# A list scheduler's durations, landing times and DMA order in a hybrid attention block

## The chip, the cores and the metric

The kernel runs on one core of one Trainium2 chip. The metric is the device time of one execution in microseconds (us). Three runs of the kernel before gave 1061.60, 1064.79 and 1065.99 us; their median is 1064.79 us.

## The reference

One layer of a streaming encoder over 16 meta tokens and 512 frames of width 1024, in float32. The stream is normalised and multiplied by one wide matrix `w_in`; its columns feed two token mixers that run beside each other, eight heads each. What follows is cut to what is computed:

```python
proj = layer_norm(h) @ w_in                       # 1024 x 7704
q_a,k_a,v_a,f_a, q_b,k_b,v_b, a_b,b_b,z_b, gate_a,gate_b = split(proj)
# FoX: softmax attention, head dim 64, with a cumulative forget gate
logits = q_a @ k_a.T * 64**-0.5 + cum[:, None] - cum[None, :]     # cum = cumsum(log_sigmoid(f_a + b_f))
y_a = softmax(causal(logits)) @ v_a
# gated DeltaNet (GDN), head dim 128: conv of 4 taps, silu, l2 norm of q and k, then by chunks
a = strict_lower((k*beta) @ k.T * decay)          # decay = exp(gc_i - gc_j)
u, w = solve(I + a, v*beta), solve(I + a, k*beta*exp(gc))
for chunk: v_new = u - w @ state; o = q_dec @ state + attn @ v_new; state = state*g_last + k_dec.T @ v_new
y_b = rms_norm(o) * gdn_norm_w * silu(z_b)
mixed = sigmoid(gate_a) * (y_a @ w_out_a) + sigmoid(gate_b) * (y_b @ w_out_b)
h = layer_norm(ALPHA*h + mixed @ w_o)
h = layer_norm(ALPHA*h + (silu(h @ w_gate) * (h @ w_up)) @ w_down)
```

## The kernel before

**Units.** The input projection is cut into units of 128 columns of `w_in`, named after what they make: f (the gate rows of all heads), qN, kN, vN and zN of GDN head N, qaP, kaP, vaP of the FoX head pair P, and last gaI, gbI, the output gates. The units run on TensorE in a fixed order (lines 66 and 1163 to 1179): group 0 has k0 q0 f0 z0 v0 z1 k1 q1 v1 and then qa0 ka0 va0; the later groups have k, q, v, k, q, v, qa, ka, va, z, z.

**A unit's weight.** Float32 is computed as three fp32r products: x_hi and x_lo with the high part of the weight, then x_hi with its low part. Unit u's raw weight (`wr_`) is loaded by SyncE (SP) into one of three buffers; ScalarE casts it to the high part (`wh_`) and writes its negative into the low part (`wl_`); then GpSimd (POOL) issues a DMA that adds the raw weight onto `wl_`. In unit u the load of u + 3 is issued at its first step and the split of u + 1 starts at its second (the hook, lines 1266 to 1271). The low pass comes last in a unit and needs `wl_` landed.

**Side work.** Between a unit's steps the planner puts the steps of the side tasks, Python generators that yield what they wait for: the scan of the gates (ending in `rows_d` in DRAM), per GDN head `gdn_prepare` (transposes psk, psq, psm, square sums, the norm chain on VectorE, Gram products) and `gdn_decay` (row broadcasts ea and em read back from `rows_d`, masked on GpSimd by AFFINE_SELECT), per group of two heads `gdn_invert` (a substitution of 31 steps on VectorE, written to DRAM as td and read back as tm and pm), `gdn_chunk` and `gdn_finish` (GpSimd's product o), the conv taps (c_q, c_k, c_v), the FoX heads, and the gates (tg). `reload` reads the pairs y_b0 and y_b2 back from DRAM; `y_tiles` then holds the split of the mixers' outputs (ys_) for the out projections.

**What sets the order.** The planner keeps a clock per engine, `est_t`. `account` (line 168) moves it on by `spent` (line 150) for every instruction, and notes when each tile is written and read; a DMA lands `DMA_LAT + fine[0]` later. `tick` (line 627) takes the side task that is ready by these clocks, within `LOOK` and `BUSY`, until `CAP` us of TensorE are placed. `Ordered` (line 199) wraps each engine: it calls `account`, and keeps the instruction in the order in which the program is written if its engine is in `PINS` and it is not a DMA:

```python
if pinned[0] and self.name in PINS and op != "dma_start":
    tc.keep_in_program_order(ins)
```

What isn't kept so is placed by the compiler's scheduler, by its own priorities; the masks of `affine_select` and the loads and casts after the units (resid, ys_, wr_wo) are placed by it too, in both kernels.

Of the kernel before, what the change touches and what calls it, by code (L numbers as in the profile page):

```python
# [8 lines left out]
F32 = mybir.dt.float32  # L9
# [6 lines left out]
PSUM = bass.MemoryType.PSUM  # L16
DRAM = bass.MemoryType.DRAM

P = 128
# [16 lines left out]
BLK = 32  # L36
BPITCH = BLK * P + BLK

PINS = ("pe", "act", "dve", "pool")
PIN_FROM = 0  # L40
LOOK, MARGIN, CAP = 0.4, 1.0, 0.6
BUSY = {'dve': 3.0, 'act': 1.0}
LAT, SELF, DMA_LAT, DMA_FINE = 0.15, 0.13, 2.3, 2.5
RAW, SPLIT, ADD_LAT = 3, 2, 3.0
HF, LOAD_ORDER = 4, "0m1pk23q"


# [16 lines left out]

STORE_AT = 3
ORDERS = "k0 q0 f0 z0 v0 z1 k1 q1 v1 x0", "k0 q0 v0 k1 q1 v1 x0 z0 z1"
SPLIT_AT = 1
POOL_BIAS = 1.2
TAIL_AT = 1
ON_POOL, AFFINE_AT = False, 14  # L70
# [7 lines left out]
def hybrid_block(ctx, tc, x, meta_tokens, ln_in_g, ln_in_b, w_in, b_f, conv_w, a_log, dt_bias,  # L78
# [16 lines left out]

    est_t = dict.fromkeys(("pe", "act", "dve", "pool", "sp"), 0.0)
    wrote, read, ring = {}, {}, {}
    fine, stale = [0.0], set()

    def tname(v):  # L100
        t = getattr(v, "tensor", None)
# [47 lines left out]

    def spent(eng, op, out, src, many):  # L150
        if op == "dma_start":
            return 0.05
        n = free(out)
        if eng == "pe":
            if op == "transpose":
                return 2 * max(n, P) / 2400
            return (4 if src[0].dtype == F32 else 1) * max(n, free(src[0])) / 2400
        n = max([n] + [free(v) for v in src[:1]])
        if op == "memset":
            return 0.05 + 1e-3 * n  # L160
        if eng == "act" and many:
            return 0.17 + 0.85e-3 * n
        if eng == "pool":
            return 0.15 + (2.1e-3 if op.startswith("tensor") else 1e-3) * n
        n += 60 if any(v.space == PSUM for v in src[:2]) else 0
        return {"act": 0.09 + 0.85e-3 * n, "dve": 0.068 + 1.04e-3 * n}[eng]

    def account(eng, op, a, k):
        aps = [v for v in list(a) + list(k.values()) if tname(v)]
        outs = [aps[0]] + ([k["accum_out"]] if "accum_out" in k else [])  # L170
        src = [v for v in aps[1:] if v is not k.get("accum_out")]
        assert not any(tname(v) in stale for v in aps), [tname(v) for v in aps]
        begin = est_t[eng]
        for v in src:
            begin = max(begin, after(wrote, tname(v), eng, 0.0 if eng == "pe" else SELF))
        for v in outs:
            if wrote.get(tname(v), (0.0, ""))[1] != "sp" or eng != "sp":
                begin = max(begin, after(wrote, tname(v), eng), after(read, tname(v), eng))
        end = begin + spent(eng, op, outs[0], src, len(outs) > 1)
        if op == "dma_start":  # L180
            done = end + DMA_LAT + fine[0]
        else:
            done = est_t[eng] = end
        for v in outs:
            wrote[tname(v)] = max(done, wrote.get(tname(v), (0.0, ""))[0]), eng
        for v in src:
            if read.get(tname(v), (0.0, ""))[0] < done:
                read[tname(v)] = done, eng
# [10 lines left out]
    class Ordered:  # L199
# [3 lines left out]
        def __getattr__(self, op):  # L203
            fn = getattr(self.eng, op)

            def call(*a, **k):
                ins = fn(*a, **k)  # L207
                account(self.name, op, a, k)
                if pinned[0] and self.name in PINS and op != "dma_start":
                    tc.keep_in_program_order(ins)  # L210
                return ins
            return call
# [476 lines left out]
    def gdn_decay(hd):  # L689
        h = hd["h"]  # L690
        ea = gp.tile([P, NT, 2, P], F32, tag="ea", name=f"ea{h}", bufs=4)
        for i in range(2):
            src = rows_d[(1 + i) * HEADS + h, META:].rearrange("(c n) -> c n", n=P)
            sp.dma_start(ea[:, :, i, :], src.unsqueeze(0).broadcast_to([P, NT, P]))
        em = gp.tile([META, META], F32, tag="em", name=f"em{h}", bufs=2)
        sp.dma_start(em, rows_d[HEADS + h, :META].unsqueeze(0).broadcast_to([META, META]))
        yield at(rdy(ea, em), 0, "act")
        yield lambda: not busy
        busy.append(h)
        eq = gp.tile([P, NT, P], F32, tag="eq", name=f"eq{h}", bufs=1)  # L700
        act.activation(eq, ea[:, :, 1, :], AF.Exp)
        for i, op in ((0, ALU.is_gt), (1, ALU.is_ge)):
            pool.affine_select(ea[:, :, i, :], ea[:, :, i, :], [[0, NT], [1, P]], op, NEG,
                               base=0, channel_multiplier=-1)
        pool.affine_select(em, em, [[1, META]], ALU.is_gt, NEG, base=0, channel_multiplier=-1)
        yield at(rdy(ea, em), 0, "act")
        for c in range(NT):
            act.activation(ea[:, c], ea[:, c], AF.Exp, bias=neg_gc[:, c, h:h + 1])
            yield soon("act")
        act.activation(em, em, AF.Exp, bias=neg_gc[:META, 4, h:h + 1])  # L710
        hd["ea"], hd["em"], hd["eq"] = ea, em, eq
# [85 lines left out]
    def gdn_invert(g, st):  # L797
# [25 lines left out]
        sp.dma_start(td[0], t3)  # L823
        dve.tensor_copy(n3, t3.rearrange("p a b -> p b a"))
        sp.dma_start(td[1], n3)
        tv = td[:, :32].rearrange("w (i b) r n -> w b r i n", b=4)
        fine[0] = DMA_FINE
        for b, c in ((0, 0), (1, 32), (2, 0)):
# [411 lines left out]
    for u, d in enumerate(units):  # L1240
        pinned[0] = u >= PIN_FROM
        if u == STORE_AT:
            for t in range(NT):
                sp.dma_start(h_v[:, t, :], toks[t])
        if u - 2 in finishing:
            gen, ps = finishing.pop(u - 2)
            finish_now(gen, lambda: tname(ps) in freed)
        if d["name"].startswith("qa"):
            pr = int(d["name"][2:])
            drain(lambda: not pr or fox[pr - 1]["done"] == 3)  # L1250
        def low():
            if u in splitting:
                finish_now(splitting.pop(u), lambda: u in los)
            return los[u]

        ps = outs0[d["name"]] if u < 2 else gbanks(f"ps_{d['name']}")
        outs = [ps[:, i, :b - a] for i, (a, b) in enumerate(d["cols"])]
        passes = [(outs, d["cols"])]
        if u == 0:
            passes = []  # L1260
            load_unit(u + 3)
            start_split(u + 1)
        elif u == 1:
            passes = [(outs[1:], d["cols"][1:])]
        for n, (o, c) in enumerate(passes):
            def hook(j):
                if n == 0 and j == 0:
                    load_unit(u + 3)
                if n == 0 and j == SPLIT_AT:
                    start_split(u + 1)  # L1270
                tick()
            if d["name"] == "f":
                o, low = [v[:6 * HEADS] for v in o], None
            gemm(o, his[u], low, x_hi, x_lo, c, KT, hook)
        gen = d["finish"](ps)
        finishing[u] = gen, ps
        start(gen, 0)
        advance(side[-1])
# [585 lines left out]
```

## Time and profile before

| what | value |
|---|---|
| median of three runs | 1064.79 us (1061.60 to 1065.99) |
| profiled execution: time, span, granted clock | 1062.41 us, 1060.7 us, 0.987 |
| busy TensorE (PE) | 989.1 us, 93% |
| busy VectorE (DVE) | 694.9 us, 66% |
| busy ScalarE (ACT) | 504.4 us, 48% |
| busy GpSimd (POOL) | 335.4 us, 32% |
| DMA | 131.03 MB, 124 GB/s on average |
| chain that ended last | PE 51%, DVE 24%, DMA 9%, issue 8%, ACT 5%, POOL 2% |

The time is that of the whole execution, the span goes from its first to its last instruction. PE busy for 93% says that it stands still for 7% of the span. The chain is followed back from the last instruction, at each step to what released it. A granted clock of 1.0 is TensorE's upper level (2.4 GHz), 0.5 its lower one (1.2 GHz). The units run from 31 to 560 us; out projections, the first layer norm, the FFN and the last norm follow.

### The profile page before, as it was taken

The numbers are of one execution on the slowest core, as the hardware profiler recorded it, in microseconds if no ns is written. First come the engines' busy times: TensorE is split into PE (matmuls) and PEld (weight loads), VectorE is DVE, ScalarE is ACT, GpSimd is POOL, SyncE is SP. The second block draws the span as 40 slices with busy tenths as digits, with TensorE's granted clock in tenths as the row PEclk, the third lists the DMA queues.
The fourth block names the chain that finished last, engine by engine and source line by source line (L and its number), as shares of the span: only waits on it lengthen the run. The fifth ranks groups of instructions, "written<-read, shape, count | busy, mean of one in ns | idle before, by whom it ended". The sixth has DMA issues, their size and how long they took to land.

```text
span 1060.7 us, 17731 instructions
## 1 busy us (share of the span) xinstructions
PE 989.1 (93%) x6765; PEld 881.9 (83%) x6765; DVE 694.9 (66%) x1467; ACT 504.4 (48%) x1031; POOL 335.4 (32%) x359
## 2 busy tenths in 40 slices
PE   5988999999989899999999999879999999999995
PEld 4887998779878898876877887679999999988884
DVE  6446586369837884780246546788989998964435
ACT  6466667455744577544463224434444435531121
POOL 5213211212130223011028002674555645235005
PEclk9999999999989999999999999999999999999998
DMA  7587656537653576457685335104243342344222
GB/s 222 132 181 168 141 111 129 135 67 173 155 122 69 125 179 140 105 138 173 162 214 151 111 100 159 41 2 118 80 120 105 95 120 81 100 136 142 84 77 79
DMA packets 170577, 131.03 MB, mean 124 GB/s; under 512 B 19708, under 2 KB 151068, under 8 KB 170492
## 3 DMA queue, kind: packets, MB, share of 16 engines
q1 hardware_dynamic: 161788, 98.39, 33.0%
q0 software_dynamic: 8704, 31.51, 15.6%
q8 instruction: 53, 0.87, 0.3%
q14 instruction: 32, 0.26, 0.1%
HBM read 90.90 MB, written 8.57 MB: 94 GB/s over the span
## 4 chain that ended last, share of the span: by engine, by line
PE 51%; DVE 24%; DMA 9%; issue 8%; ACT 5%; POOL 2%; SPq 0%; DVEq 0%; POOLq 0%; ACTq 0%
PE d L1366 3%; PE d L1364 3%; PE d L1365 3%; PE ps_v L207 3%; DVE wlo_b L1428 3%; PE ptm L207 3%; PE ps_ga L207 2%; PE ps_q L207 2%; PE ps_z L207 2%; PE ps_gb L207 2%; PE ps_va L207 2%; DMA wl_ga<-wr_ga 2%; PE po L1321 2%; PE o L240 2%; PE po L1319 2%
## 5 line engine op out<-in xcount | busy, mean ns | idle before, releaser
L285 DVE TENSOR_TENSOR wl_d<-wr_d,wh_d 128x1024 fp32r<-128x1024 f32 x18 | 29.6, 1643 | 45.2 <-ACT wh_d L283 45.2
L283 ACT CAST wh_d<-wr_d 128x1024 fp32r<-128x1024 f32 x18 | 18.9, 1050 | 66.5 <-PE d L1366 44.6
L1482 POOL TENSOR_TENSOR wr_a<-wr_a,sums 128x512 f32<-128x512 f32 x22 | 29.2, 1329 | 66.3 <-DVE wl_a L1428 66.2
L207 DVE TENSOR_TENSOR t<-t,tmp 34x31 f32<-34x31 f32 (+15 forms) x124 | 42.8, 345 | 2.1 <-DVE tmp L207 0.2
L207 DVE TENSOR_TENSOR tmp<-n,t 34x31 f32<-34x31 f32 (+15 forms) x124 | 41.9, 338 | 2.8 <-DMA n<-nd 0.9
L1476 POOL TENSOR_TENSOR sums<-wr_a,spare_raw 128x512 f32<-128x512 f32 x11 | 14.7, 1335 | 81.4 <-DVE stats L240 70.9
L1365 PE MATMUL d<-wl_d,f_h 128*128 128x512 f32 (+1 forms) x104 | 39.7, 381 | 0.0
L1364 PE MATMUL d<-wh_d,f_h 128*128 128x512 f32 (+1 forms) x104 | 39.6, 381 | 0.0
L1448 PE MATMUL pa<-v_h,wh_a 128*128 128x256 f32 x160 | 39.3, 279 | 0.0
L1448 PE MATMUL pa<-v_h,wl_a 128*128 128x256 f32 x160 | 39.1, 279 | 0.0
L1667 ACT ACTIVATE res<-res 128x512 f32<-128x512 f32 x11 | 7.0, 634 | 62.1 <-DVE res L1728 62.1
L240 POOL TENSOR_SCALAR rst_l<-rsy_l,ve_l 128x1 f32<-128x1 f32 x21 | 10.8, 514 | 73.0 <-DVE rsy_l L240 71.6
L1428 DVE TENSOR_TENSOR wlo_b<-wr_b,whi_b 128x1024 fp32r<-128x1024 f32 x11 | 22.6, 2054 | 16.4 <-ACT whi_b L1427 16.4
L283 ACT CAST wh_wo<-wr_wo 128x512 fp32r<-128x512 f32 (+1 forms) x16 | 13.3, 836 | 40.9 <-PE po L1320 13.8
L285 DVE TENSOR_TENSOR wl_wo<-wr_wo,wh_wo 128x512 fp32r<-128x512 f32 (+1 forms) x16 | 22.3, 1405 | 15.8 <-ACT wh_wo L283 15.8
L1448 PEld LDWEIGHTS pa<-v_h,wh_a 128*128 128x128 f32 x160 | 30.2, 188 | 0.0
L1448 PEld LDWEIGHTS pa<-v_h,wl_a 128*128 128x128 f32 x160 | 30.0, 187 | 0.0
L207 DVE SCALAR_TENSOR_TENSOR r<-ks,nbeg,bv 128x128 f32<-128x128 f32 x32 | 11.2, 351 | 28.6 <-PE ks L207 23.4
L207 ACT COPY o<-ks 128x128 f32<-128x128 f32 x32 | 8.5, 266 | 44.2 <-DVE r L207 44.2
L1448 PE MATMUL px<-v_h,rb 128*128 128x256 f32 x176 | 25.5, 289 | 2.9 <-ACT v_h L240 2.9
L1448 PE MATMUL px<-v_h,wlo_b 128*128 128x256 f32 x88 | 22.7, 293 | 5.8 <-DVE wlo_b L1428 5.8
L1427 ACT CAST whi_b<-spare_raw 128x1024 fp32r<-128x1024 f32 x10 | 10.5, 1052 | 35.4 <-PE pd L1448 35.4
(791 smaller groups left out, 3696.7 us busy)
## 6 DMA issues: line engine op xcount, KB each, us to landing
wr_d<-in_w_down_dram SPq DMA_DIRECT2D x18, 512.0 KB, 3.8
spare_raw<-in_w_gate_dram SPq DMA_DIRECT2D x11, 512.0 KB
wr_b<-in_w_up_dram SPq DMA_DIRECT2D x11, 512.0 KB, 3.9
wr_a<-in_w_gate_dram SPq DMA_DIRECT2D x11, 512.0 KB
wr_a<-in_w_up_dram SPq DMA_DIRECT2D x11, 512.0 KB, 5.6
wr_k<-in_w_in_dram SPq DMA_DIRECT2D x8, 512.0 KB, 7.0
wr_q<-in_w_in_dram SPq DMA_DIRECT2D x8, 512.0 KB, 4.3
wr_z<-in_w_in_dram SPq DMA_DIRECT2D x8, 512.0 KB, 5.7
```

Source lines behind the costliest of these rows:

```text
L207: ins = fn(*a, **k)
L240: return lambda *a, **k: tc.keep_in_program_order(fn(*a, **k))
L283: nc.scalar.copy(hi[:, :k * n], raw[:, :k * n])
L285: eng.tensor_sub(lo[:, :k * n], raw[:, :k * n], hi[:, :k * n].bitcast(F32))
L1319: nc.tensor.matmul(g[:, j, :], wh[:, i, :], hi[i], start=i == 0, stop=False)
L1321: nc.tensor.matmul(g[:, j, :], wl[:, i, :], hi[i], start=False, stop=i == k - 1)
L1364: nc.tensor.matmul(acc, ah, wh[:, cols], start=kk == 0, stop=False)
L1365: nc.tensor.matmul(acc, ah, wl[:, cols], start=False, stop=False)
L1366: nc.tensor.matmul(acc, al, wh[:, cols], start=False, stop=kk == ktiles - 1)
L1428: order(eng.tensor_sub(lo, src, hi.bitcast(F32)))
L1448: order(nc.tensor.matmul(dst, a[:, k, :], v[i][:, k, :], start=n == 0, stop=n == 11))
L1482: pin(nc.gpsimd.tensor_sub(v1[:, 1], v1[:, 1], sums[:, 0]))
```

## The change

The constants, the two duration functions, the place of a load in its unit, the list of engines held in program order, one wait and one landing time are changed:

```diff
-PINS = ("pe", "act", "dve", "pool")
+PINS = ("pe", "act", "dve", "pool", "sp")
-LAT, SELF, DMA_LAT, DMA_FINE = 0.15, 0.13, 2.3, 2.5
-RAW, SPLIT, ADD_LAT = 3, 2, 3.0
+LAT, SELF, DMA_LAT, DMA_FINE, DMA_ROWS, SWITCH = 0.15, 0.02, 2.3, 3.2, 6.0, 0.1
+RAW, SPLIT, ADD_LAT = 3, 2, 3.4
-SPLIT_AT = 1
+SPLIT_AT, LOAD_AT = 1, 12
     def spent(eng, op, out, src, many):
         if op == "dma_start":
-            return 0.05
+            return 0.85 if eng == "pool" else 0.45
         n = free(out)
         if eng == "pe":
+            full = op == "transpose" or src[0].dtype == F32
+            switch = SWITCH if full != pe_full[0] else 0.0
+            pe_full[0] = full
             if op == "transpose":
-                return 2 * max(n, P) / 2400
-            return (4 if src[0].dtype == F32 else 1) * max(n, free(src[0])) / 2400
+                return switch + max(n, P) / 1175
+            return switch + (2 * max(n, free(src[0])) / 1150 if full else max(n, free(src[0])) / 2195)
         n = max([n] + [free(v) for v in src[:1]])
         if op == "memset":
-            return 0.05 + 1e-3 * n
-        if eng == "act" and many:
-            return 0.17 + 0.85e-3 * n
+            return 0.05 + 0.9e-3 * n
+        if eng == "act":
+            return (0.28 if many else 0.09) + 0.9e-3 * n
         if eng == "pool":
-            return 0.15 + (2.1e-3 if op.startswith("tensor") else 1e-3) * n
-        n += 60 if any(v.space == PSUM for v in src[:2]) else 0
-        return {"act": 0.09 + 0.85e-3 * n, "dve": 0.068 + 1.04e-3 * n}[eng]
+            return 0.15 + (2.1e-3 if op.startswith("tensor_t") or op in ("tensor_add", "tensor_sub", "tensor_mul") else 1e-3) * n
+        return 0.14 + 1.0e-3 * n
...
         if op == "dma_start":
             done = end + DMA_LAT + fine[0]
+            est_t[eng] = end
...
-                if pinned[0] and self.name in PINS and op != "dma_start":
+                if pinned[0] and self.name in PINS:
                     tc.keep_in_program_order(ins)
...
             src = rows_d[(1 + i) * HEADS + h, META:].rearrange("(c n) -> c n", n=P)
+            fine[0] = DMA_ROWS
             sp.dma_start(ea[:, :, i, :], src.unsqueeze(0).broadcast_to([P, NT, P]))
+            fine[0] = 0.0
...
         sp.dma_start(td[1], n3)
+        yield at(rdy(td) - MARGIN)
...
-                if n == 0 and j == 0:
+                if n == 0 and j == LOAD_AT:
                     load_unit(u + 3)
```

So the DMAs that the planner issues on SyncE and GpSimd are kept in the order of the program, those clocks move on with each, and all its other choices are made with the new durations. What this does to the order of the instructions is shown at four places (the number at a name's end only tells tiles apart).

GpSimd from the adding DMA of z1's weight on, before (wl_ is a weight's low part, ea0 to ea2 the decay tiles of heads 0 to 2, gt3 a scratch tile of the gates, nm0 a small tile of head 0):

```order
L207 DMA wl_z1_596<-wr_z1_462 128x1024
L207 MEMSET gt3_523 128x120
L207 DMA wl_k1_676<-wr_k1_517 128x1024
L207 AFFINE_SELECT ea0_706<-ea0_706 128x4x128
L207 AFFINE_SELECT em0_709<-em0_709 16x16
L207 DMA wl_q1_760<-wr_q1_591 128x1024
L207 AFFINE_SELECT ea1_1011<-ea1_1011 128x4x128
L207 AFFINE_SELECT ea0_706<-ea0_706 128x4x128
L207 AFFINE_SELECT em1_1014<-em1_1014 16x16
L207 DMA wl_v1_866<-wr_v1_670 128x1024
L207 MEMSET nm0_930 32x32
L207 AFFINE_SELECT ea2_1678<-ea2_1678 128x4x128
```

and after (qf0 is the query tile of head 0):

```order
L210 DMA wl_z1_594<-wr_z1_496 128x1024
L210 MEMSET gt3_520 128x120
L210 AFFINE_SELECT ea0_682<-ea0_682 128x4x128
L210 DMA wl_k1_721<-wr_k1_574 128x1024
L210 AFFINE_SELECT em0_685<-em0_685 16x16
L210 DMA wl_q1_765<-wr_q1_621 128x1024
L210 AFFINE_SELECT ea0_682<-ea0_682 128x4x128
L210 DMA wl_v1_866<-wr_v1_736 128x1024
L210 MEMSET nm0_926 32x32
L210 DMA wl_qa0_942<-wr_qa0_820 128x1024
L210 TENSOR_TENSOR qf0_500<-qf0_500,eq0_832 128x512
L210 AFFINE_SELECT ea1_1005<-ea1_1005 128x4x128
```

One mask of ea0 has moved ahead of the adding DMA of k1, the masks of ea1 have moved behind that of qa0, and those of ea2 are no longer among these rows.

TensorE around the transposes of head 4, before (psk4, psm4 and psq4 are banks of PSUM, ps_q5 that of unit q5):

```order
L207 MATMUL ps_q5_3234<-x_lo_128,wh_q5_3149 128x268 x2
L207 MATMUL ps_q5_3234<-x_hi_127,wh_q5_3149 128x268 x2
L207 MATMUL psk4_3286<-ident_107,k4T_3067 128x128 x4
L207 MATMUL psm4_3288<-ident_107,k4T_3067 16x128
L207 MATMUL psq4_3287<-ident_107,qf4_3154 128x128 x4
L207 MATMUL ps_q5_3234<-x_lo_128,wh_q5_3149 128x268 x2
```

and after (ps_k5 is the bank of unit k5, which runs ahead of q5):

```order
L210 MATMUL ps_k5_3160<-x_hi_127,wh_k5_3091 128x268 x2
L210 MATMUL ps_k5_3160<-x_lo_128,wh_k5_3091 128x268 x2
L210 MATMUL psk4_3216<-ident_107,k4T_3087 128x128 x4
L210 MATMUL psm4_3218<-ident_107,k4T_3087 16x128
L210 MATMUL psq4_3217<-ident_107,qf4_3156 128x128 x4
L210 MATMUL ps_k5_3160<-x_hi_127,wh_k5_3091 128x268 x2
```

The transposes have moved forward by one unit.

SyncE around the reload of the mixer's output (y_b0_again, y_b2_again), before:

```order
L207 DMA wr_gb0_5274<-in_w_in_dram 128x8x128
L207 DMA wr_ga1_5485<-in_w_in_dram 128x8x128
L207 DMA wr_gb1_5674<-in_w_in_dram 128x8x128
L207 DMA y_b0_again_6570<-y_d_132 128x1024
L207 DMA y_b2_again_6572<-y_d_132 128x1024
L207 DMA wr_ga2_5752<-in_w_in_dram 128x8x128
```

and after (wr_wo is a weight of the out projections, resid the residual stream):

```order
L210 DMA wr_gb6_6349<-in_w_in_dram 128x8x128
L210 DMA wr_ga7_6419<-in_w_in_dram 128x8x128
L1310 DMA resid0_6620<-h_d_129 128x1024
L210 DMA wr_gb7_6464<-in_w_in_dram 128x8x128
L210 DMA y_b0_again_6570<-y_d_132 128x1024
L210 DMA y_b2_again_6572<-y_d_132 128x1024
L275 DMA wr_wo0_0_6639<-in_w_out_a_dram 128x4x128
L1310 DMA resid2_6628<-h_d_129 128x1024
L275 DMA wr_wo1_0_6657<-in_w_out_b_dram 128x8x128
```

The two loads have moved from between the gate weights gb1 and ga2 to behind the last one, gb7.

ScalarE near the end of the units, before (tg12 is the tanh of the gate unit ga6, ys_ the split outputs):

```order
L207 CAST wh_gb6_6438<-wr_gb6_6299 128x1024
L207 ACTIVATE wl_gb6_6439<-wh_gb6_6438 128x1024
L1296 CAST ys_o_14_6591<-y_b6_5487 128x512
L207 ACTIVATE tg12_6479<-ps_ga6_6433 128x512
L207 CAST wh_ga7_6482<-wr_ga7_6364 128x1024
L1296 CAST ys_pm_12_6590<-y_b6_5487 128x512
L207 ACTIVATE wl_ga7_6483<-wh_ga7_6482 128x1024
```

and after:

```order
L210 CAST wh_gb6_6448<-wr_gb6_6349 128x1024
L1302 CAST ys_o_14_6591<-y_b6_5521 128x512
L210 ACTIVATE wl_gb6_6449<-wh_gb6_6448 128x1024
L1302 CAST ys_qf_0_6580<-y_b0_again_6570 128x512
L210 ACTIVATE tg12_6479<-ps_ga6_6445 128x512
L210 CAST wh_ga7_6482<-wr_ga7_6419 128x1024
L1302 CAST ys_kt_2_6582<-y_b0_again_6570 128x512
L210 ACTIVATE wl_ga7_6483<-wh_ga7_6482 128x1024
L1302 CAST ys_kn_4_6584<-y_b2_again_6572 128x512
```

Two casts of the reloaded tile y_b0_again now stand between the split of gb6 and that of ga7, one of them ahead of the tanh of ga6.

## Rows read from the trace of the kernel before

**Rows 1.** Window (us, engines' busy us (xcount), PEclk, DMA share, GB/s), the planned stretch

```profile
31.00:560.00 529.00, 497.45 (x3667) 441.37 (x3666) 315.43 (x959) 306.10 (x733) 107.45 (x165) 0.99 0.63 141
```

**Rows 2.** The same view, three windows behind the stops at 293 us

```profile
292.00:296.00 4.00, 1.74 (x12) 1.35 (x12) 3.88 (x7) 3.03 (x6) 2.60 (x6) 0.95 0.87 170
296.00:300.00 4.00, 2.32 (x36) 2.12 (x37) 1.33 (x3) 1.28 (x3) 0.87 (x1) 0.50 0.81 141
300.00:304.00 4.00, 3.86 (x30) 3.63 (x31) 0.88 (x2) 1.28 (x5) 2.17 (x2) 0.69 0.94 211
```

**Rows 3.** Waits of PE, 31 to 560 us (engine, line, waited for: total, times, longest)

```profile
PE ps_ka L207 <- DVE nm L207: 3.2, 1, 3.2
...
PE oT L207 <- POOL o L207: 2.7, 1, 2.7
PE ps_qa L207 <- DVE c_q L207: 2.6, 1, 2.6
PE ps_q L207 <- DMA wl_q<-wr_q: 2.5, 1, 2.5
PE w L207 <- DMA tm<-td: 2.1, 1, 2.1
PE ps_va L207 <- DVE q_stack L207: 1.8, 1, 1.8
PE ps_qa L207 <- DMA wl_qa<-wr_qa: 1.7, 1, 1.7
```

**Rows 4.** Timeline of POOL (start us, us, what, [idle before <-releaser])

```profile
65.18 0.97 POOL L207 TENSOR_SCALAR_AFFINE_SELECT ea<-ea 128x512 f32<-128x512 f32 x1 [6.81 <-DMA ea<-rows_d]
...
68.34 0.89 POOL L207 DMA_DIRECT2D wl_q<-wr_q  x1 [0.38 <-DMA wr_qa<-in_w_in_dram]
```

**Rows 5.** Timeline of SP, the loads of the first broadcast

```profile
59.51 2.55 SPq L207 DMA_DIRECT2D ea<-rows_d  x2
```

**Rows 6.** The chain that ended last, by time (start us, us, what)

```profile
42.02 7.93 DMA wl_v<-wr_v
...
57.50 5.37 DMA wl_k<-wr_k
...
249.18 6.02 PE ps_v L207 x48
...
468.52 5.57 PE ps_ga L207 x24
...
540.96 7.31 DMA wl_ga<-wr_ga
...
553.78 6.15 DMA wl_ga<-wr_ga
```

**Rows 7.** Timeline of ACT, the first square of a head

```profile
283.93 0.28 ACT L207 ACTIVATE scr<-psk 128x128 f32<-128x128 f32 x1 [0.41 <-PE psm L207]
```

**Rows 8.** Timeline of DVE, starts of two norm chains and the conv taps

```profile
269.87 0.17 DVE L207 TENSOR_SCALAR ss<-ss 128x9 f32<-128x9 f32 x1 [0.64 <-ACT scq L207]
...
276.51 1.56 DVE L207 SCALAR_TENSOR_TENSOR c_v<-ps_v,prm,c_v 128x528 f32<-128x528 f32 x2
...
287.51 0.17 DVE L207 TENSOR_SCALAR ss<-ss 128x9 f32<-128x9 f32 x1 [2.67 <-ACT scq L207]
```

**Rows 9.** Timeline of SP, the reload and the last gate weight

```profile
449.05 0.82 SPq L207 DMA_DIRECT2D y_b_again<-y_d  x2
...
548.28 0.38 SPq L207 DMA_DIRECT2D wr_gb<-in_w_in_dram  x1
```

**Rows 10.** The tile y_b_again (durations in ns), and its landing

```profile
L1296 ACT CAST ys_qf<-y_b_again x1: 611/611/611, 530.1 to 530.1; 128x512 fp32r<-128x512 f32 x1
...
DMA to landing us min/median/max: 4.5/4.5/4.5
```

**Rows 11.** Timeline of ACT, one half of a split

```profile
475.67 1.06 ACT L207 ACTIVATE wl_ga<-wh_ga 128x1024 fp32r<-128x1024 f32 x1
```

**Rows 12.** Waits of all engines, 31 to 560 us, columns as in rows 3

```profile
POOL ea L207 <- DMA ea<-rows_d: 35.1, 8, 8.1
```

More of the change, by code (lines that the diff above doesn't have):

```diff
@@ L97, in hybrid_block @@
     wrote, read, ring = {}, {}, {}
-    fine, stale = [0.0], set()
+    fine, stale, pe_full = [0.0], set(), [False]
     def tname(v):
```

## The prediction

> **What bounds the kernel now.** I read the profile from the outside in. The busy table of the whole span says that TensorE works 93% of 1060.7 us, so the kernel can only become shorter where TensorE stands still or runs at half clock. The windows by stage then say where the change can reach at all: its planner orders the stretch from about 31 to 560 us, and there TensorE is busy for 497.45 of 529.00 us [rows 1]. So 31.6 us of standstill is all that a better order can win, plus what the clock loses. The clock is one more term: after the pair of stops at 293 and 295 us the granted clock falls to the lower level (1.2 of 2.4 GHz) and the three windows there lose (1 - 0.95), (1 - 0.50) and (1 - 0.69) of 4 us each, 3.4 us together [rows 2].
>
> Then the list of waits, for TensorE alone, gives the standstill by what ended it [rows 3]. The seven that I use are single stops of 1.7 to 3.2 us, and they have three kinds of causes: a low part of a weight that lands late (wl_q, wl_qa), a bank of PSUM that VectorE frees late (nm, c_q, q_stack), and a tile that GpSimd makes late (o). For each I looked in the timelines of GpSimd, SyncE, ScalarE and VectorE at what the late engine had been doing.
>
> **The change, part by part.** No matmul is added or removed: between the gate rows and the out projections there are 3,108 in both orders, and they change between fp32 and fp32r work 324 times before and 320 times now. What changes is who stands before whom.
>
> *The row broadcasts and GpSimd.* GpSimd masks a head's decay tile ea and issues the adding DMA of every weight. Before, it stood from 58.4 to 65.18 us for the first broadcast, was held again by em0, and only then issued wl_q [rows 4]: TensorE paid 2.5 us for wl_q. Later the masks of ea2 and ea3, loaded far ahead, stood before wl_qa, and TensorE paid 1.7 us there and 3.2 us at ka0 [rows 3]. Now ea1 to ea3 are loaded later and their masks are gone from in front of wl_qa: 4.9 us go. What is late next is wl_ka0, which stands behind ea1's mask: ea1's load stands on SyncE behind wr_va0, and a broadcast needs 5.7 us from its first issue to the mask (59.51 to 65.18) [rows 4, 5]; I put its adding DMA about 2 us later than ka0's low pass wants it. Net -3.0 us; bounds 0 (the wait is as long as what went) and -4.9.
>
> The first mask has also moved ahead of wl_k1. The rows are now turned before unit z1, not in it, and ScalarE copies them before a conv and a split, so I take the first broadcast 3.5 us earlier, at 56 us, the mask done at 62.5, and wl_k1 some 5 us later than its 57.50 us. It landed 5.37 us after that [rows 6], so now at about 67.5 us, some 2.5 us after k1's high pass ends. In exchange wl_q1 no longer waits. I count the two even, from -2.5 to +2.5.
>
> *The stores of h_d.* They stand now behind wr_z1, which waits for the gate weights, so they run at 33 to 44 us, beside wl_z0. An adding DMA beside another load took 7.93 us (wl_v) and alone 5.37 (wl_k) [rows 6]. Against that, wl_v, which TensorE waited for before, loses its company. Even, 0 to +2.5.
>
> *The GDN steps and VectorE.* The planner now charges VectorE, ScalarE and the DMAs nearer to what they take, and places the steps of a head earlier. Before, psk4 stood in q5 at its 23rd matmul; the norm chain of that head ran on VectorE before the conv taps of q5, and qa2 waited 2.6 us for the bank; the next chain held q_stack, and va2 waited 1.8 us, then 2.1 us for the inverse's tiles tm [rows 3]. With the 3.4 us of the clock [rows 2] this corner cost 9.9 us. Now psk4 stands in k5 and psk5 in v5. From the first square on ScalarE to the start of the chain it takes 3.6 us (283.93 to 287.51), from there through the chain and the three taps 6.6 us (269.87 to 276.51) [rows 7, 8]: 10.2 us. Behind psq4 stand 32 matmuls of k5 and 48 of q5, at 6.02 / 48 = 0.125 us each [rows 6], 10.0 us: about 0.5 us late with v4T between. Behind psq5 stand 16 of v5 (2.0 us) and all of qa2 (5.57 us by a gate unit) [rows 6], 7.6 us: 2.6 us late at ka2. The inverse starts its DMAs about a unit and a half earlier and has them in time. So 9.9 go and 3.1 come: -6.8 us; bounds -9.9 and 0 (the late chain of psk5 takes the clock down as well).
>
> *GpSimd's product o.* At 359 us TensorE waited 2.7 us for o2 [rows 3], because GpSimd stood for two broadcasts ahead of it. Now o2 and o3 stand before those masks: -2.7 us; bounds 0 and -2.7.
>
> *The reload of y_b.* This is the term against the change. Two heads' pairs were read back at 449.05 us, long before use. Now their place is where they are written, behind wr_gb7, which SyncE issued at 548.28 us [rows 9], just as wl_ga6 had landed (540.96 + 7.31) [rows 6]. On ScalarE the cast of y_b0 stands now ahead of ga6's tanh and of the split of ga7. A reload took 4.5 us to land [rows 10], so the earliest is 553.2 us, and up to 2 us more behind wr_gb7's own bytes. Then ScalarE does two casts and a tanh of about 0.61 us and the two halves of the split at 1.06 us [rows 10, 11]: 3.9 us, and wl_ga7 starts at 557.1 to 559.1, not 553.78 us [rows 6]. TensorE waited for it before already, so all of it is lost: +3.3 to +5.3, I take +4.5; the upper bound, with the reload as slow as wl_v's 7.93 us, is +6.8; the lower one is 0, were the split to go by.
>
> In the Trainium skill, "DMA: Bandwidth & Descriptors", section "Anatomy of one DMA — SWDGE (gpsimd) path", a wait on a semaphore is spent on the issuing sequencer before dispatch, while the DMA engines only empty their queues. GpSimd's row at 68.34 agrees: wl_q went out after the masks, not when its data were ready. By that rule every DMA now held in order also holds those behind it, and the two masks' rival below is what it would make of this kernel.
>
> *Nothing by itself.* The 12th step moves only the place of a weight's load among SyncE's DMAs: its issue is set by the buffer, as wr_gb7's is. Its cover is the three raw buffers; without it a late load costs what wl_q cost, 2.5 us. The yield behind td lets loads pass SyncE's wait for td, which no row shows TensorE to pay.
>
> Sum: -3.0 - 6.8 - 2.7 + 4.5 = -8.0 us; the 15 us of stops that I couldn't tie to an edit stay. The span goes from 1060.7 to 1052.7, the profiled time (1062.41, 1.7 us around the span) to 1054.4. The median of the runs shown is 2.4 us above that execution, so I forecast **1057 us**. Adding the bounds: all the gains at their best and no reload, 1064.8 - 4.9 - 9.9 - 2.7 - 2.5 = 1045; all gains at nothing and costs at their top, 1064.8 + 2.5 + 2.5 + 6.8 = 1077.
>
> **Rivals.**
>
> *Masks ahead of the weights (slower).* In the new order one mask stands ahead of each of wl_k1, wl_ka0, wl_k3, wl_va1, wl_q5, wl_ka2, wl_v7 and wl_va3. GpSimd waited 35.1 us in 8 such waits before [rows 12], 4.4 us each, and TensorE paid about 10 of it. If each of the eight costs TensorE 2.4 us, that is 19 us, of which 4.5 are already counted: +14.7 on -8.0, 1071 us. It decides from about 1.6 us each. For it: ea loads now start later and so land nearer to their mask. Against: at wl_k3 and wl_ka2 more than a whole unit stands between the mask and the low pass.
>
> *The stops only move (no change).* A head's chain takes its 10.2 us wherever it stands, and a bank is freed behind it. If the corner at 274 to 300 us is paid elsewhere (-6.8 becomes 0) and the reload costs 4.5: -1.2, so 1064 us. For it: 2.6 us of it I already found at ka2.
>
> *The planner is right (much faster).* If of the 15 us left over half goes too, and no reload stall: -8.0 - 4.5 - 7.5 gives 1045 us. Against: the masks and the split of y_b are not held by the planner.
>
> **Numbers.** Forecast 0.40, no change 0.25, masks 0.15, much faster 0.20. A difference under 0.5% (5.3 us) can't be told from none here. Of the forecast's own spread (1051 to 1063) I give two thirds to faster; with the much faster case that is 0.27 + 0.20, rounded to faster 0.48; same 0.13 + 0.20, 0.32; slower 0.20 with the tail of no change. The range that leaves out a tenth on each side is 1044 to 1070.
>
> **What would show it.** Right: no wait over 1 us at qa0, at qa2 and va2, and at oT2; the clock at 1.00 through the inverse of group 1; a stop of 3 to 5 us at ga7's low pass with ScalarE waiting for y_b. Right in part: about 2.5 us at k1 and ka2, 2 us at ka0. Wrong: GpSimd's masks followed by stops of TensorE at most weights, or a standstill of TensorE in the stretch that is again 30 us.

## The result, and the profile after

The changed kernel takes 1103.94 us (median of four runs, 1093.06 to 1109.93) against 1065.39 us before: 1.035 times as long, interval 1.027 to 1.042. I had forecast 1057. It is 38.6 us slower, outside the range. The highest of the four runs counts as a slow one; the other three have a median of 1099.77 us, 34 us above before, and the differences below start from that.

Its profiled execution took 1099.77 us, with a span of 1098.0 us and a granted clock of 0.971 (0.987 before). Windows of the changed kernel, columns as in rows 1: first from 31 us to the low pass of ga7 (559.97 us before, 589.95 us now), then the rest of the units:

```profile
31.00:590.00 559.00, 511.43 (x3667) 452.23 (x3666) 317.75 (x956) 303.74 (x728) 107.58 (x164) 0.96 0.60 135
590.00:606.00 16.00, 8.65 (x31) 6.34 (x30) 6.81 (x5) 6.04 (x9) 11.64 (x6) 0.81 0.68 179
```

Against [rows 1] the first row is the whole lesson in arithmetic. The same 3667 matmuls are busy for 511.43 us and not 497.45: 14.0 us more, at a mean clock of 0.96 and not 0.99. And TensorE stands still for 47.6 us and not 31.6: 16.0 us more. That is 30 of the 37.3 us between the two spans. The rest arises at the end of the units. There gb7's low pass began 5.7 us after ga7's before, and 13.3 us after it now. First TensorE's row of the kernel before:

```profile
565.65 2.02 PE L207 MATMUL ps_gb<-x_hi,wl_gb 128*128 128x512 f32 x8
```

and the low passes of gb6, ga7 and gb7 in the changed kernel, the first and the last behind a wait (the last row is cut where its window ends, at 606 us):

```profile
584.28 2.11 PE L210 MATMUL ps_gb<-x_hi,wl_gb 128*128 128x512 f32 x8 [3.25 <-DMA wl_gb<-wr_gb]
...
589.95 2.02 PE L210 MATMUL ps_ga<-x_hi,wl_ga 128*128 128x512 f32 x8
...
603.29 2.93 PE L210 MATMUL ps_gb<-x_hi,wl_gb 128*128 128x512 f32 x6 [6.46 <-DMA wl_gb<-wr_gb]
```

TensorE's waits of the changed kernel, 31 to 606 us, columns as in rows 3:

```profile
PE ps_gb L210 <- DMA wl_gb<-wr_gb: 9.7, 2, 6.5
PE ps_ka L210 <- DVE c_v L210: 5.6, 2, 3.0
PE w L210 <- ACT tm L210: 4.3, 1, 4.3
PE ps_va L210 <- DVE q_stack L210: 4.2, 2, 2.4
PE ps_k L210 <- DMA wl_k<-wr_k: 3.8, 3, 1.7
PE ps_qa L210 <- DMA wl_qa<-wr_qa: 3.5, 1, 3.5
PE ps_ga L210 <- DMA wl_ga<-wr_ga: 2.6, 1, 2.6
PE s L210 <- DMA k_rest<-cum_d: 2.2, 1, 2.2
```

The stops of [rows 3] have gone, but for the first, and as many others have come, at other units: wl_qa is now qa1's, q_stack va1's and va3's, and tm is a step further on, in the inverse of group 2. The first one, at ka0, is still there, 3.03 us behind VectorE's conv taps c_v:

```profile
92.93 0.48 PE L210 MATMUL ps_ka<-x_hi,wh_ka 128*128 128x264 f32 x2 [3.03 <-DVE c_v L210]
```

The clock falls behind such stops, as it did in [rows 2], but in nine places and not three. Not every stop does it: behind the 3.03 us at ka0 and the 3.25 us at gb6 the granted clock stayed at 1.00. The longest is behind the inverse of the last group, where TensorE is busy without a break and has half the clock for some 14 us (windows of the changed kernel):

```profile
517.00:521.00 4.00, 2.44 (x55) 1.67 (x55) 0.00 (x0) 3.11 (x6) 0.87 (x1) 1.00 0.66 138
521.00:525.00 4.00, 4.00 (x23) 3.17 (x22) 0.69 (x1) 0.97 (x3) 0.00 (x0) 0.54 1.03 225
525.00:529.00 4.00, 4.00 (x22) 2.70 (x21) 0.00 (x0) 2.18 (x4) 0.00 (x0) 0.50 0.52 140
529.00:533.00 4.00, 4.00 (x11) 2.81 (x12) 0.69 (x1) 1.66 (x3) 0.87 (x1) 0.50 0.54 113
533.00:537.00 4.00, 4.00 (x16) 2.84 (x15) 0.00 (x0) 0.43 (x2) 0.00 (x0) 0.75 0.96 257
```

### The profile page after: what moved, and what is told of

It is laid out like the page before. It is cut to its first block, busy times and chain, and to the rows that moved or that the text cites. A ratio compares the mean times of both kernels' runs of the same rounds, so it can differ in the third digit from the quotient of the medians.

```text
span 1098.0 us, 17718 instructions
## 1 busy us (share of the span) xinstructions
PE 1003.9 (91%) x6765; PEld 892.6 (81%) x6765; DVE 696.3 (63%) x1467; ACT 506.5 (46%) x1031; POOL 334.9 (31%) x359
## 3 DMA queue, kind: packets, MB, share of 16 engines
q1 hardware_dynamic: 161788, 98.39, 31.6%
## 4 chain that ended last, share of the span: by engine, by line
PE 49%; DVE 24%; issue 10%; DMA 8%; ACT 5%; POOL 2%; SPq 0%; DVEq 0%; POOLq 0%; ACTq 0%
PE ps_q L210 4%; PE o L243 3%; PE d L1372 3%; PE d L1370 3%; PE d L1371 3%; DVE wlo_b L1434 3%; PE ps_ga L210 3%; PE ps_gb L210 2%; PE ptm L210 2%; PE po L1327 2%; PE po L1325 2%; PE po L1326 2%; PE ps_v L210 2%; PE ps_k L210 2%; DVE wl_a L1434 2%
## 5 line engine op out<-in xcount | busy, mean ns | idle before, releaser
L210 POOL TENSOR_SCALAR_AFFINE_SELECT ea<-ea 128x512 f32<-128x512 f32 x16 | 11.9, 747 | 57.4 <-DMA ea<-rows_d 51.0
L1335 DVE SCALAR_TENSOR_TENSOR mx<-tg,po 128x512 f32<-128x512 f32 x16 | 10.3, 684 | 28.9 <-PE po L1327 28.9
L210 PE MATMUL ps_gb<-x_hi,wh_gb 128*128 128x512 f32 x64 | 27.3, 427 | 0.9 <-ACT wh_gb L210 0.9
```

## The experiments

Three theories stood at the start. O: the held order of the DMAs costs. D: the new durations place the steps worse. L: the 12th step brings the weights late. Each run's ratio is to the kernel before on the same chip.

**e1, the durations alone.** After, with the held DMAs, the 12th step and the wait behind td taken back:

```diff
-SPLIT_AT, LOAD_AT = 1, 12
+SPLIT_AT, LOAD_AT = 1, 0
...
-                if pinned[0] and self.name in PINS:
+                if pinned[0] and self.name in PINS and op != "dma_start":
...
-        yield at(rdy(td) - MARGIN)
```

> The kernel before with the new durations and landing times alone (the clocks of SyncE and GpSimd move with each DMA too, but their DMAs are not held in order; loads at the first step, no wait behind td). After is 38 us slower than before (1104 against 1065). Theory O (the held order of the DMAs is what costs): 1060 to 1068 us, TensorE's standstill between 31 us and the end of the units about 40 us as before. Theory D (the new durations place the side steps worse, above all the inverses and the norm chains): 1088 to 1096, the 38 less the 10 to 12 us at the two last gate units that the reload of y_b costs. Theory L (the loads at the 12th step): as before, 1065.

Measured: 1065.26 us, 1.0013 (0.9990 to 1.0035): no difference. D falls.

**e2, the held order alone.** Before, with "sp" added to PINS and `and op != "dma_start"` dropped.

> The kernel before with the DMAs of SyncE and GpSimd held in program order, and nothing else. Theory O: 1090 to 1104 us. Theory D: 1065 plus the tail alone, 1073 to 1078, with the wait for wl_gb at the last unit as in after (6.5 us). Theory L: as theory D.

Measured: 1121.56 us, 1.056 (1.052 to 1.060): 57 us, more than the whole change. The expected wait for the last wl_gb is not there; TensorE waited 11.1 us for wh_va and 9.6 for wh_ka instead.

**e3, after without held DMAs.** Only e1's change to the line with PINS.

> After, with the DMAs of SyncE and GpSimd left to the compiler's scheduler again; durations, 12th step and the wait behind td stay. The reload of y_b can then be issued early again, so the tail (10 to 12 us at gb6 and gb7) goes under each theory. Theory O: 1062 to 1070. Theory D: 1090 to 1095. Theory L: 1090 to 1095 too (the loads' place in the program would matter little when they float, so at the low end).

Measured: 1083.78 us, 1.0205 (1.015 to 1.026): between O and D. TensorE's order is that of after, so holding costs this plan 16 us; the 12th step and the wait behind td together cost 19 on top of e1.

**e4, after with the load at the first step.** Only `LOAD_AT` from 12 to 0.

> After, with a unit's load issued at its first step again (12 to 0); the rest of the change stays. Theory L: the waits for wl_qa, wl_k, wl_z, wl_ga go, some 12 us and the clock behind them, 1080 to 1088. Theories O and D: 1098 to 1106, since the load waits for its buffer anyway, at whichever step it stands.

Measured: 1091.37 us, 1.027 (1.023 to 1.032). Between the theories again, and 8 us less than after, so each edit was then put on e1 by itself.

**e5, the durations with the 12th step.** e1 with `LOAD_AT` = 12.

> Durations with loads at the 12th step; no DMA is held in order, and there is no wait behind td. Durations alone took 1065 us, with the 12th step and the wait behind td 1084. Theory L2 (the 12th step makes those 19 us: the weights' raw loads go out later or the planner shifts its splits): 1080 to 1088. Theory Y (the wait behind td makes them: the inverses' tiles come later): 1063 to 1068. Theory C (either small edit only re-deals the planner's order, and any such deal is worth plus or minus 10 us): anything between, 1070 to 1080.

Measured: 1081.11 us, 1.0155 (1.012 to 1.020). e3, which has the wait behind td besides, is 2.7 above that, and the intervals do not tell this from nothing. (That wait also gives TensorE another order, so the 2.7 is not the price of waiting.) The 12th step it is, though not by the load's place: a kernel that issues the load at the 12th step and lets the planner count it at the first has the row order of e1 on four engines and differs in one row of SyncE; the other way round it has e5's. With floating DMAs, only the planner's reckoning moved. (Read from the orders; neither was run.)

**e6 and e7, one queue held.** e1 with SyncE's DMAs held (e6), and with GpSimd's held (e7):

```diff
+                if pinned[0] and self.name in PINS and (op != "dma_start" or self.name == "sp"):
```

> Durations alone (loads at the first step, no wait behind td), with SyncE's DMAs held in program order, GpSimd's not. Theory S (the held queue that costs is SyncE's: a store of ea onto nd, which waits for Gram products, stands ahead of the weights' loads and the broadcasts): 1082 to 1092 us, SyncE waiting over 40 us in all for ea (8 in the kernel with the durations alone), and the tail's 6 us wait for the last wl_gb. Theory G (GpSimd's held adding DMAs cost): 1066 to 1072.

> Durations alone, with GpSimd's adding DMAs held in program order, SyncE's not. Theory S: 1062 to 1070 us. Theory G: 1080 to 1092, with wl_ waits on TensorE above 15 us in all.

Measured: e6 1083.84 us, 1.0187 (1.014 to 1.023); e7 1063.82 us, 1.0004 (0.997 to 1.004). So it is SyncE's queue. About GpSimd's, e7 says little: its program differs from e1's in one place, the adding DMA of ga0 and a product o that stand next to each other have changed places. Unheld, GpSimd's DMAs stand in almost the held order already. But e6's end had no wait of 6 us for wl_gb; ga7's wl_ga cost 3.8 there, so that part of the expectation was wrong.

e6 also tells what the wait behind td does with the load at the first step. e4 and e6 have the same orders on TensorE, VectorE and ScalarE; e4's SyncE has one load (ka2's) some rows earlier, and its GpSimd that one pair exchanged. e4 took 8 us longer, with intervals that just touch (1.0233 is the end of both).

**e8, after with the reload free.** TensorE's order is the same row by row:

```diff
-                if pinned[0] and self.name in PINS:
+                if pinned[0] and self.name in PINS and "_again" not in str(tname(a[0])):
```

> After, with only the two reloads of y_b left out of SyncE's held order, so that the compiler's scheduler places them some 60 us earlier; TensorE's order is the same row by row. The tail's share by the trace of after: the waits of 3.25, 0.9 and 6.46 us at gb6 and gb7 against 0.6 and 1.5 at the same place before. Theory T (that stall is the price of the reload's place): 10 to 12 us less than after, 1092 to 1094. Theory N (wl_gb is late there for another reason, the loads of the residual stream and the out weights beside it): within 3 us of after, 1101 to 1106.

Measured: 1087.34 us, 1.021 (1.016 to 1.027): 12.4 us less than after, 12.9 by the two profiled spans (1098.0 and 1085.1). This is 3.6 us from e3, which holds nothing: in after, the reload is most of what the held order costs.

**e9 to e12 and e15, e16, controls.** Two of the planner's numbers are moved a little: LAT, its allowance from one engine to the next, to 0.16 us in e1, in e5 and in before (e9, e11, e12) and to 0.14 in e7 (e15); MARGIN, its margin at the time when a tile is ready, to 1.05 us in e1 (e10) and to 0.95 in e7 (e16). Each gives a new order, called a deal below, since it is dealt anew without a reason in the chip.

> Control: the new durations alone (1065 us), with the planner's allowance between engines at 0.16 instead of 0.15 us, a change of 0.01 us that says nothing of the chip. It changes about 2,800 lines of TensorE's order, as many as the 12th step does. Theory C (any change of the planner's numbers deals the order anew, and a deal is worth 10 us and more either way): 1050 to 1085, off 1065 by over 5. Theory L2 (the 12th step costs by what it says, a later landing): within 4 us of 1065.

> The durations with the 12th step (1081 us), the allowance at 0.16 instead of 0.15. Theory C: it falls anywhere in 1055 to 1090, and the mean of the two deals with the 12th step is not clearly above that of the deals without it. Theory L2: 1077 to 1085, above every deal without the 12th step.

> Control: the kernel before (1065 us), the allowance at 0.16 instead of 0.15 and nothing else. Theory C, with the kernel before being one of its better deals: 1065 to 1090. Theory D' (the old durations give an order that is good by itself): within 4 us of 1065.

> Another deal of the order: durations, GpSimd held (1064 us), the allowance between engines at 0.14 instead of 0.15 us. Theory C: 1055 to 1080, most likely above 1064, since 1064 is among the lowest of the deals so far (1064 to 1081). If one of these two beats the kernel before it is by chance of the deal.

> Control: the new durations alone, with the margin behind a ready time at 1.05 instead of 1.0 us. Theory C: off 1065 by over 5 us, to either side. Theory L2: within 4 us of 1065.

> As the run before, with the margin at 0.95 instead of 1.0 us and the allowance at 0.15: 1055 to 1080, most likely above 1064.

Measured, with the kernels whose order they vary:

| kernel | us | ratio and interval |
|---|---|---|
| before (medians beside the runs) | 1063.5 to 1065.5 | |
| before, LAT 0.16 (e12) | 1075.06 | 1.012 (1.008 to 1.016) |
| durations (e1) | 1065.26 | 1.001 (0.999 to 1.004) |
| durations, LAT 0.16 (e9) | 1073.47 | 1.010 (1.007 to 1.012) |
| durations, MARGIN 1.05 (e10) | 1069.94 | 1.006 (1.004 to 1.007) |
| durations, 12th step (e5) | 1081.11 | 1.016 (1.012 to 1.020) |
| durations, 12th step, LAT 0.16 (e11) | 1068.49 | 1.004 (1.002 to 1.007) |
| durations, GpSimd held, LAT 0.14 (e15) | 1086.16 | 1.021 (1.018 to 1.024) |
| durations, GpSimd held, MARGIN 0.95 (e16) | 1075.44 | 1.012 (1.008 to 1.016) |

A hundredth of a microsecond in LAT moves about as much of TensorE's order as the 12th step does (1,178 to 1,546 changed lines of 6,231 instructions, against 1,528) and the time by 8 to 22 us, mostly up, once down. With LAT at 0.15 the 12th step costs 16 us (e5 against e1); with LAT at 0.16 it gains 5 (e11 against e9). So those 16 us are what this one order is worth, not what the step does; and the kernel before is, with e1, the lowest of nine orders, 1064 to 1086 (e3's, at 1084, is a tenth; e7's order of TensorE is e1's).

**e13 and e14, all held but the reload.** e8's edit on e2 (old durations) and on e1 with both queues held.

> The order alone (1122 us, the old durations), with the two reloads of y_b left out of the held order. Theory T (the reload's place is what holding the order costs): 1122 less 12 to 17, 1105 to 1110, if the rest of the 57 us is something else; 1068 if the tail were all of it. Theory S (a DMA that waits holds the weights' loads behind it, as at the waits of 11.1 and 9.6 us for wh_va and wh_ka, where the planner had counted no time for SyncE's DMAs): 1104 to 1112, with those two waits still there.

> The new durations with all DMAs of SyncE and GpSimd held in order but for the two reloads of y_b; loads at the first step, no wait behind td. TensorE's order is that of the durations alone (1065 us), row by row. Theory T (once the planner counts SyncE's time, the reload is all that the held order costs): 1063 to 1070. Theory S (SyncE's waits for ea, over 60 us in all against 8, cost besides): 1075 to 1082.

Measured: e13 1121.17 us, 1.053 (1.050 to 1.056); e14 1083.56 us, 1.019 (1.016 to 1.022). Neither moved from its kernel with the reload held (e2 and e6), so the reload's price hangs on the order too: 12 us in after, nothing measurable here. With the load at the first step the held order costs something else. e14 has e1's orders on TensorE, VectorE and ScalarE, so the trace shows where. SyncE in e14, and its wait there:

```profile
378.83 0.37 SPq L210 DMA_DIRECT2D wr_qa<-in_w_in_dram  x1
379.25 1.13 SPq L210 DMA_DIRECT2D ea<-rows_d  x2
380.43 0.50 SPq L210 DMA_DIRECT2D em<-rows_d  x1
```

```profile
SPq L210 <- DMA wl_k<-wr_k: 6.4, 1, 6.4
```

and ScalarE and TensorE behind it:

```profile
386.41 0.63 ACT L210 ACTIVATE eq<-ea 128x512 f32<-128x512 f32 x1 [10.97 <-DMA ea<-rows_d]
386.94 1.03 ACT L210 CAST wh_q<-wr_q 128x1024 fp32r<-128x1024 f32 x1
...
388.02 0.81 PE L210 MATMUL ps_q<-x_hi,wh_q 128*128 128x268 f32 x2 [6.34 <-ACT wh_q L210]
```

The broadcast of ea was ready to go (with its place free, in e17 below, it went out at 328.12), but the weight load of qa3 ahead of it waited 6.4 us for a raw buffer, until an adding DMA had landed. The broadcast followed at 379.25, and ScalarE began the exponential eq 7.2 us later, after standing for 10.97 us; the split of q7, next in ScalarE's order, came late; and TensorE waited 6.34 us. A second such place is at v5 (7.9 us on ScalarE, 5.7 on TensorE). The waits of ScalarE for ea tell the kernels apart. In order, each from its own trace: e2, e4, e14, after, e18 (below).

```profile
ACT eq L207 <- DMA ea<-rows_d: 72.7, 8, 19.1
```

```profile
ACT eq L210 <- DMA ea<-rows_d: 19.8, 4, 9.3
```

```profile
ACT eq L210 <- DMA ea<-rows_d: 20.6, 3, 11.0
```

```profile
ACT eq L210 <- DMA ea<-rows_d: 2.5, 2, 2.0
```

```profile
ACT eq L207 <- DMA ea<-rows_d: 1.1, 1, 1.1
```

**e17 and e18, the broadcasts free.** e14 and e2, with the loads of ea and em left out of the held order as well (in e2 the reload stays held). The orders of TensorE, VectorE and ScalarE stay the same row by row:

```diff
-                if pinned[0] and self.name in PINS and "_again" not in str(tname(a[0])):
+                if pinned[0] and self.name in PINS and "_again" not in str(tname(a[0])) and not (op == "dma_start" and tname(a[1]) == tname(rows_d)):
```

> The run with the durations and held DMAs (1083.6 us, the reload free), with the loads of the row broadcasts ea and em left out of SyncE's held order too; the orders of TensorE, VectorE and ScalarE are the same row by row. Theory H (a broadcast stands on SyncE behind a weight load that waits for its buffer, then ScalarE's eq waits for ea, by 7.9 us at 264 and 11.0 us at 386, and the split and the conv behind it on ScalarE make TensorE wait): the stops of 5.7 us at v5 and 6.3 us at q7 go, 1064 to 1070 us. Theory N (the held order costs by other DMAs, the stores of ea and the loads of tm and pm): 1079 to 1086.

> The order alone (1122 us, old durations), with the loads of ea and em left out of the held order. Theory H: the stops of 11 us at va1 (where ScalarE waited 19.1 us for ea) and 10 us at ka3 go, and those for scq and bv with them; 1068 to 1080 us. Theory N: 1110 to 1124.

Measured: e17 1062.08 us, 0.9963 (0.9938 to 0.9988); e18 1078.40 us, 1.012 (1.006 to 1.017). 21.5 us of e14's time go, and 43 of e2's 57. Theory H holds; some 13 us of e2's cost stay (the reload is still held there), and no run splits them. In e17 SyncE issued the broadcasts of heads 6 and 7 long before, ScalarE's eq of the same head ran with no wait, and the split of q7 behind it:

```profile
328.12 2.15 SPq L210 DMA_DIRECT2D ea<-rows_d  x4
...
371.47 0.62 ACT L210 ACTIVATE eq<-ea 128x512 f32<-128x512 f32 x1
371.99 1.04 ACT L210 CAST wh_q<-wr_q 128x1024 fp32r<-128x1024 f32 x1
```

e17 is faster than before and after: by 0.4% (0.1 to 0.6) against before, less than a deal moves. Against e1, whose orders on TensorE, VectorE and ScalarE it shares, it is 0.5%, and the intervals do not overlap. It is the best kernel of this study; whether holding the rest of the DMAs helps in another order wasn't tried.

## Why the prediction was wrong

**The sum of stops.** The step that failed is "the 15 us of stops that I couldn't tie to an edit stay". I took each edit's gain from the stops of one execution of one order and let the rest stand. The controls show that any change of the planner's numbers makes a new order whose stops are elsewhere. Of nine orders with floating DMAs or GpSimd's alone held, the one I started from was among the two lowest; their mean is 1073 us. The forecast for "the order is new, I know nothing more" was about 1% slower, before any cost of the held queue. "The stops only move" was among the rivals, at 1064; it was right in kind and too good in size. In the terms of the sum: the 12.5 us of gains came to nothing in e1, which has all the durations and no held DMA; the 12th step, put at nothing, measured 16 in this order; the reload, put at 4.5, measured 12 (e8).

**The clock.** I counted its fall as part of one corner, 3.4 us [rows 2], to be won. (That counts half-clock time in which TensorE stood still as lost; by its busy 1.74, 2.32 and 3.86 us in those windows I estimate 2.4.) It was a cost behind nine of the new stops: the same 3667 matmuls took 14.0 us longer. How much of that is the order's is less sure than it looks. e1 and e7 have one order but for a pair on GpSimd; their windows from 31 us to the same low pass of ga7, e1 first:

```profile
31.00:564.40 533.40, 506.61 (x3660) 451.23 (x3658) 317.70 (x959) 306.65 (x732) 106.55 (x165) 0.96 0.62 140
```

```profile
31.00:557.69 526.69, 500.24 (x3663) 445.24 (x3663) 316.77 (x959) 304.69 (x731) 105.79 (x164) 0.98 0.62 141
```

TensorE stands still for 26.8 and 26.5 us there, some 5 less than before: the durations did shorten the waits. It is busy 9.2 us longer than before in e1 and 2.8 in e7; the clock fell in seven places in the one and in three in the other. So up to 6 us of busy time lie between two executions, on two chips, of one order. The trace of before is a favourable one as well: its execution was granted 0.987, the 64 executions of before beside e1 to e18 had 0.975 to 0.984, 0.980 on average. After's four had 0.962 to 0.972, so most of its loss stands; e1's ten had 0.977 on average, hardly less than before's.

**The reload.** The first half of the mechanism was right: SyncE issued it behind wr_gb7, and ScalarE had its casts ahead of a tanh and of splits and stood 4.52 us for them. The stop was not where I had put it. I expected it at ga7's low pass, 4.5 us, at most 6.8; that pass began at 589.95 without a wait. TensorE stood 3.25 us at gb6's and 0.90 and 6.46 at gb7's, and the reload's price is 12 us by e8. ScalarE in the changed kernel:

```profile
579.34 0.62 ACT L1302 CAST ys_qf<-y_b_again 128x512 fp32r<-128x512 f32 x1 [4.52 <-DMA y_b_again<-y_d]
...
581.81 1.06 ACT L210 ACTIVATE wl_ga<-wh_ga 128x1024 fp32r<-128x1024 f32 x1
...
589.73 0.62 ACT L286 CAST wh_wo<-wr_wo 128x512 fp32r<-128x512 f32 x1 [5.45 <-DMA wr_wo<-in_w_out_a_dram]
...
591.79 1.03 ACT L210 CAST wh_gb<-wr_gb 128x1024 fp32r<-128x1024 f32 x1
```

The chain of the changed kernel shows what I had missed. The adding DMAs of gb6 and gb7 land in over 9 us (7.31 and 6.15 for ga6 and ga7 in [rows 6]), the first beside the reload's two loads, the second beside loads of the residual stream and an out weight:

```profile
575.12 9.12 DMA wl_gb<-wr_gb
...
594.20 9.04 DMA wl_gb<-wr_gb
```

In e8, with the reload free, gb6's went out at 571.38, and the buffer that it frees was taken again 5.1 us later. gb6's low pass waited for the first. So did SyncE, 10.0 us, for the raw buffer that gb6 leaves; only then, at 584.29, could it issue the first out weight:

```profile
SPq L275 <- DMA wl_gb<-wr_gb: 10.0, 1, 10.0
```

The cast of that weight stands on ScalarE ahead of gb7's split and waits 5.45 us. So the delay passes a second time, to gb7. In e8 gb6's low pass does not wait at all, ga7's waits 0.81 us and gb7's does not.

**The row broadcasts.** At qa0 and q1 the stops went as predicted, and wl_k1's new one is 1.28 us (I had bounded it at 2.5). The 3.2 us at ka0, most of the 4.9 us that this term was to give, did not go: 3.03 us are left. There the norm chain and the taps c_v stand on VectorE in both kernels; the chain starts 6.9 us earlier (85.65 us, 92.58 before), but TensorE comes to ka0 earlier too. So the 3.2 us that I had put down to the masks were not to be had by moving them.

And I followed the broadcasts to GpSimd's masks alone, and the rival on the slow side was built there: masks ahead of eight weights, 1071 us. GpSimd did wait longer for ea (51.0 us in 8 waits against 35.1 in [rows 12]), but TensorE's waits for low parts of weights, apart from the 9.7 us of gb6 and gb7, came to 11.0 us in all, against 10.4 before. The place where a held broadcast costs is ScalarE's eq, which stands ahead of a split. In after that is small (2.5 us): where e4 has 19.8 with the load at the first step, the load at the 12th stands behind the broadcast. In that one respect the step that I costed at nothing "by itself" mends the held queue; that is read from the two traces, whose orders differ in other things too, and e4 as a whole is 8 us faster than after.

The rule that I quoted from the Trainium skill, "DMA: Bandwidth & Descriptors", section "Anatomy of one DMA — SWDGE (gpsimd) path", that a wait is spent on the issuing sequencer, pointed the right way. SyncE's rows at 378.83 and 379.25 in e14 agree with it, for the other kind of queue: the broadcast went out right behind the load that had waited 6.4 us.

**What was right.** The waits at qa0, qa2 and va2, the 2.7 us at o2, and tm's wait at group 1 are gone. VectorE's late chain was predicted to cost 2.6 us at ka2, and did; that it fits to a tenth is luck, since it was added up from four rounded lengths. TensorE's row there:

```profile
298.05 0.48 PE L210 MATMUL ps_ka<-x_hi,wh_ka 128*128 128x264 f32 x2 [2.60 <-DVE c_v L210]
```

Most local readings were sound (not those at ka0 and ga7), and their sum was worth little.

**The account.** From 1065: the durations 0 (e1); the 12th step 16 (e5), as this order falls; the wait behind td 3, not told from 0 (e3); the rest of the held order 3.6 (e8 against e3), not told from 0; the reload in the held queue 12.4 (e8 against after). Together 1100; they add up because each is the difference of two neighbours on one path, and another path would share the sum out otherwise. What stays open is which trait of an order makes it good: idle time and the granted clock both differ among the nine, and no single stop explains them. Open too is why e4 takes 8 us more than e6.

## What to carry to other kernels

Where a list scheduler sets the order, first measure what a change that means nothing does (here 5 to 22 us, up to 2%): the kernel before sat at the low end of its deals, and an edit of the planner's numbers is better forecast from their mean. (That it sat there because it was kept for its time is a guess; e1, a fresh deal, sits there too.) When a queue is put in order, look for its short DMA with an early reader that stands behind a long one waiting for a buffer, and follow the reader's own queue to the bound engine: broadcasts behind such loads cost 18 us here (e14 against e1), and leaving the broadcasts alone out of the order gave them back. Ask also what a moved load lands beside: the reload slowed an adding DMA, and that was paid twice, at the weight's own low pass and by the buffer that it frees.

## What was not expected of the hardware

After a stop of 1.4 us among the small matmuls of the last inverse, TensorE had the lower level of its clock for some 14 us while it was busy without a break (the windows from 517 to 537 us); behind the stops at 293 and 295 us before it was back within 8 [rows 2]. With the same order of TensorE, e3 stood 3.67 us at that inverse and then had the lower level for some 19 us; e8 did not stop there, and its clock did not fall. An adding DMA of 512 KB took 9.1 us to land beside the reload's two loads; in the kernel before, the quickest of the seven of the k units took 4.5:

```profile
DMA to landing us min/median/max: 4.5/4.7/7.7
```

The 5.37 us of [rows 6], which I had taken for the time alone, ran beside the first broadcast's loads, issued at 59.51 [rows 5].
